# A second product of the output phase as seven inner products: A22 in blocks 2 to 6, with left sums formed a phase earlier

## The chip, the cores and the metric

The kernel runs on one core of a Trainium2 chip. The metric is the device time of one execution in microseconds. The engines are named as in the profile: PE is TensorE (matmuls; PEld its weight loads), DVE VectorE, ACT ScalarE, POOL GpSimd, SP the engine that issues most DMAs. All data are float32.

## The reference

Of the two kinds of layer that the reference knows, DEPTH = 1 leaves one: the pooling mixer, with a residual, and the final norm. x is (1, 4096, 1024).

```python
normed = rms_norm(x, norm_w)
u, gate = jnp.split(normed @ in_w, 2, axis=-1)
ug = u.reshape(b, s, 4, 256)
pooled = jnp.stack([trailing_mean(ug[:, :, g], w)
                    for g, w in enumerate((2, 4, 8, 16))], axis=2) - ug
mixed = jnp.einsum('bsgc,gcd->bsgd', pooled, group_w) + group_b
y = mixed.reshape(b, s, 1024) * scale * jax.nn.silu(gate)
h = x + y @ out_w
return rms_norm(h, final_norm_w)
```

`trailing_mean` is the mean over the last `window` tokens, fewer at the start.

## The kernel before

**Stages.** The map of each group is first multiplied into `in_w` (line L419 of the profile). Then come three phases. The first input phase ("a") takes 4 blocks of 1024 tokens and computes u and gate for channel groups 0 and 1; the second ("b") takes the same blocks for groups 2 and 3. Behind each half of a block's products `pool` forms the trailing means by a scan on VectorE, multiplies by scale, bias and gate, and stores the result y to DRAM (`yd`). The output phase ("o") takes 8 blocks of 512 tokens: y @ out_w, plus x, then the final norm and the store.

**Products.** Each matrix product of a block is cut into 2 x 2 parts and done by Winograd's form of Strassen's scheme, in seven products P1 to P7 instead of eight; the outer scheme's left sums are formed on VectorE and its right sums are formed beforehand. In the output phase they run in the order P1, P7, P6, P2, P5, P4, P3. A left factor (A11, A12, A21, A22 and sums of them) is 256 tokens by 512 channels, the right factor 512 by 512. P2 is A12 times B21; P4's left factor is A22.

**Split operands.** Every float32 factor is split into a high part, written by a ScalarE copy (L182), and a low part, the rest, by a VectorE subtract (L168). A pair of factors takes three matmuls (`mm3`, L636): high-high, high-low, low-high. One output product is 2 row halves x 4 parts of K x 3 = 24 matmuls of 128x512, the first 12 into one PSUM bank, the others into a second. The split left factors stand in a ring of four buffers, `op`.

**The inner scheme.** From block `FIRST_INNER` = 2 on, P2 is itself done as seven products of quarter size (`mm_inner`, L756): 7 x 6 = 42 matmuls of 128x256. The first, A11 x B11 of the inner scheme, stands between the two halves of P6 (`inner_first`), the other six in P2's place (`inner_rest`). The inner left sums S1 to S4 are four VectorE operations of 128x256, formed in `split_o` just before their split. The inner right sums T1 to T4 are formed by eight VectorE operations of 128x256 (`form_inner`, L168) from two raw loads, and split into slots that are retired for them (`split_inner`, tiles `inner_T`), all in block 1. `add_quarter` (L764) adds the inner products to the result on VectorE, 128x256 each.

**PSUM.** Eight banks in four sets of two: x, v, y and a free set. P1 and P2 go to x, P7 and P4 to v, P6, P5 and P3 to y; the sets change roles from block to block. `evict_o` adds a finished bank to the rows `hs` on VectorE (L1101, 128x512 an add), or, for P1, copies x into y on ScalarE. P5 writes the y banks that P6 used, with P2 between them.

**The final norm.** After P4 and after P3 `finish` squares the rows on ScalarE (L990), takes a root there, the reciprocal on VectorE (L229), and one Newton step on GpSimd (L225, L241, L242, L243, L246, all 128x2), and scales on VectorE (L994, 128x1024 each). Block 7 has a path of its own.

**What sets the order.** Each engine runs its instructions in the order in which the loop at the end of the builder issues them, held back where `tc.issue_after` says so. For step n the loop issues loads up to four products ahead (`load_reach`) on SP's queue, splits up to two ahead (`split_reach`), pooling that is due (the last two poolings fall into output block 0), then the product and its evictions. Data stand in 11 `st` and 8 `vt` slots of 128x1024 (and x2); `take` hands out the one that has been free longest.

```python
order of one step:  load -> split -> pool_due -> run (product, evict) -> load_inner, form_inner, split_inner
```

## Time and profile before

| | us |
|---|---|
| Median of 3 runs (908.23 to 908.53) | 908.41 |
| The profiled execution | 908.96 |
| Span of its trace | 907.2 |
| Output phase's first matmul of the inner scheme | 698.68 |
| End of the last matmul | 897.77 |

One more thing is worth knowing when the rows are read: DVE is VectorE, and a row such as `op<-vt,op` gives the tile written and the tiles read. The page's slices show how the load lies in time:

```profile
PE   9999999999999999999999999999999999999997
DVE  5999994894998996586696598589978888788877
POOL 0022102001100000000000000000002001001000
```

Each digit is the busy share of a fortieth of the span (22.7 us), in tenths. GpSimd has next to nothing to do from the middle of the first input phase until output block 0.

### The profile page before, as it was taken

How to read it: one execution, taken by the hardware profiler on the slowest of the kernel's cores; microseconds unless marked ns; L12 is line 12 of the kernel's file. 1: busy time of each engine (PE TensorE's matmuls, PEld its weight loads, DVE VectorE, ACT ScalarE, POOL GpSimd, SP SyncE). 2: the span in 40 equal slices, each digit the busy share in tenths (PEclk: the TensorE clock that was granted, in tenths of full speed). 3: DMA queues.
4: the chain of work that ended last, by engine and by line, in shares of the span. 5: the costliest groups of instructions: out<-in, count | busy, mean ns of one | idle time of the engine just before them, and what ended most of it. 6: DMA issues, size and time to landing. Idle time of an engine off the chain costs nothing.

```text
span 907.2 us, 11594 instructions
## 1 busy us (share of the span) xinstructions
PE 899.5 (99%) x4338; PEld 791.1 (87%) x4338; DVE 737.2 (81%) x858; ACT 471.9 (52%) x766; POOL 55.4 (6%) x129
## 2 busy tenths in 40 slices
PE   9999999999999999999999999999999999999997
PEld 7888888888888888888888888888888898898996
DVE  5999994894998996586696598589978888788877
ACT  6879547447346565256345546654435435344344
POOL 0022102001100000000000000000002001001000
PEclk9999999999999999999999999999999999999999
DMA  9984966756756535016614625745665374363332
GB/s 350 408 314 157 344 218 207 262 188 227 276 213 239 221 124 203 22 49 230 255 46 167 264 96 177 249 155 193 214 204 187 114 257 163 142 229 135 122 139 94
DMA packets 63048, 178.09 MB, mean 196 GB/s; under 512 B 6096, under 2 KB 22864, under 8 KB 62992
## 3 DMA queue, kind: packets, MB, share of 16 engines
q1 hardware_dynamic: 56496, 156.09, 47.7%
q10 hardware_dynamic: 4176, 13.65, 4.0%
q0 software_dynamic: 2320, 7.62, 2.5%
q8 instruction: 34, 0.56, 0.2%
q14 instruction: 22, 0.18, 0.1%
HBM read 116.50 MB, written 60.83 MB: 195 GB/s over the span
## 4 chain that ended last, share of the span: by engine, by line
PE 98%; DVE 1%; issue 0%; ACT 0%; DVEq 0%; ACTq 0%
PE bank L636 91%; PE bank L756 3%; PE bank L419 3%; PE bank L1208 0%; DVE w L168 0%; DVE op L168 0%; DVE st L168 0%; PE bank L485 0%; DVE vt L1073 0%; ACT vt L1021 0%; DVE vt L1101 0%; DVE st L1101 0%; ACT vt L182 0%; DVE columns L1051 0%; DVEq L1585 0%
## 5 line engine op out<-in xcount | busy, mean ns | idle before, releaser
L636 PE MATMUL bank<-op,w 128*128 128x512 f32 x2688 | 581.3, 380 | 0.1
L636 PEld LDWEIGHTS bank<-op,w 128*128 128x128 f32 x2688 | 508.6, 189 | 72.3 <-ACT early L182 0.6
L636 PE MATMUL bank<-w,op 128*128 128x512 f32 (+1 forms) x1212 | 261.2, 377 | 0.0
L636 PEld LDWEIGHTS bank<-w,op 128*128 128x128 f32 x1212 | 226.9, 189 | 30.8
L168 DVE TENSOR_TENSOR op<-st,op 128x1024 fp32r<-128x1024 f32 x124 | 150.9, 1220 | 67.8 <-ACT op L182 67.7
L182 ACT ACTIVATE op<-st 128x1024 fp32r<-128x1024 f32 x124 | 130.2, 1053 | 121.0 <-PE bank L636 83.0
L182 ACT ACTIVATE vt<-bank 128x512 f32<-128x512 f32 x98 | 55.9, 592 | 51.0 <-PE bank L636 38.7
L182 ACT ACTIVATE op<-vt 128x1024 fp32r<-128x1024 f32 x48 | 50.1, 1052 | 48.3 <-PE bank L636 22.1
L168 DVE TENSOR_TENSOR st<-st,st 128x1024 f32<-128x1024 f32 (+2 forms) x55 | 60.7, 1116 | 8.2 <-DMA st<-sd 3.3
L168 DVE TENSOR_TENSOR op<-vt,op 128x1024 fp32r<-128x1024 f32 x48 | 58.3, 1221 | 8.4 <-ACT op L182 8.3
L182 ACT ACTIVATE bank<-bank 128x512 f32<-128x512 f32 (+1 forms) x60 | 32.0, 537 | 53.0 <-PE bank L636 37.1
L1101 DVE TENSOR_TENSOR st<-bank,st 128x512 f32<-128x512 f32 x58 | 39.5, 686 | 8.0 <-PE bank L636 7.9
L225 POOL TENSOR_SCALAR oms<-oss 128x2 f32<-128x2 f32 x14 | 8.7, 620 | 591.2 <-ACT st L990 558.1
L168 DVE TENSOR_TENSOR st<-st,vt 128x1024 f32<-128x1024 f32 (+1 forms) x35 | 39.3, 1153 | 0.2
L168 DVE TENSOR_TENSOR vt<-bank,vt 128x512 f32<-128x512 f32 (+1 forms) x51 | 33.6, 681 | 6.8 <-PE bank L636 6.8
L168 DVE TENSOR_TENSOR w<-st,w 128x1024 fp32r<-128x1024 f32 x22 | 26.6, 1223 | 12.3 <-ACT w L182 12.3
L825 DVE TENSOR_TENSOR_SCAN vt<-vt,bf 128x512 f32<-128x512 f32 x28 | 34.5, 1269 | 0.2 <-ACT vt L182 0.2
L182 ACT ACTIVATE w<-st 128x1024 fp32r<-128x1024 f32 x22 | 22.9, 1052 | 17.4 <-PE bank L636 15.0
L182 ACT ACTIVATE st<-bank 128x512 f32<-128x512 f32 x32 | 18.8, 594 | 25.0 <-PE bank L636 17.8
L168 DVE TENSOR_TENSOR vt<-vt,vt 128x1024 f32<-128x1024 f32 (+1 forms) x28 | 30.7, 1102 | 1.0 <-DMA vt<-rd 0.9
L168 DVE TENSOR_TENSOR vt<-vt 128x1024 f32<-128x1024 f32 (+2 forms) x28 | 30.4, 1107 | 0.0
L182 ACT ACTIVATE st<-st 128x1024 f32<-128x1024 f32 x24 | 25.3, 1053 | 7.6 <-DVE st L168 5.4
(126 smaller groups left out, 619.9 us busy)
## 6 DMA issues: line engine op xcount, KB each, us to landing
st<-in_x SPq DMA_DIRECT2D x36, 512.0 KB, 4.5
st<-sd SPq DMA_DIRECT2D x28, 512.0 KB, 4.6
st<-in_xt SPq DMA_DIRECT2D x27, 512.0 KB, 7.6
vt<-in_x SPq DMA_DIRECT2D x21, 512.0 KB, 4.2
sd<-st ACTq DMA_DIRECT2D x21, 512.0 KB, 4.5
vt<-yd SPq DMA_DIRECT2D x18, 512.0 KB, 5.2
yd<-vt SPq DMA_DIRECT2D x17, 512.0 KB, 2.8
out<-st SPq DMA_DIRECT2D x17, 512.0 KB, 3.5
```

The lines of the kernel that those rows point to most:

```text
L168: made.append(nc.vector.tensor_tensor(out=dst, in0=a, in1=b, op=op))
L182: made.append(nc.scalar.activation(dst, src, func, **how))
L225: nc.gpsimd.tensor_scalar(out=ms, in0=ss, scalar1=1.0 / D, scalar2=EPS, op0=ALU.mult, op1=ALU.add)
L419: latest[0] = nc.tensor.matmul(ps2[kk][:, j * 256 : (j + 1) * 256], a[:, kk, 2 * j + t, :], maps if len(pairs) == 1 else woven(maps), star ...
L636: latest[0] = nc.tensor.matmul(ps, a, b, start=start and n == 0, stop=stop and n == 2, skip_group_check=True).ins
L756: latest[0] = nc.tensor.matmul(dst, a[k][x_], b[k][y_], start=start and k + n == 0, stop=k == 1 and n == 2, skip_group_check=True,).ins
L825: nc.vector.tensor_tensor_scan(s[:, j, at:end], v[:, j, at:end], v[:, j, at - win : end - win], sums_of[j] if sums_of else 0.0, ALU.add, A ...
L1101: partial["added"] = nc.vector.tensor_tensor(out=dst, in0=src, in1=dst, op=ALU.add).ins
```

## The change

The inner scheme is used for two products, by a table `INNER = {P2: (2, 7), P4: (2, 6)}` of first and last blocks: P4 (A22 times its right factor) becomes seven inner products in blocks 2 to 6. Its first inner product stands between the halves of P5 and uses the x banks, which P2 has left; its results go to the v banks.

- The inner left sums are no longer formed in `split_o`. `inner_sums`, called by `pool` in the second input phase, forms them from y for both products at once: four VectorE operations of 128x512 for each half block of tokens, for output blocks 2 to 7, and two stores to DRAM (`sumd`). The output phase loads them, one load of 512 KB per inner product, and splits them.
- `form_inner` runs on GpSimd: eight operations of 128x256 for each of the two weights, 16 in all. P4's are issued at the end of block 1, and split in block 2. T2 goes into the slot of the first raw load, T4 into columns of the weight itself (B12) that the inner scheme does not read. These columns are loaded and split again in block 7, where P4 is ordinary.
- The Newton step of the output rows: one operation is left on GpSimd, three go to VectorE (`factors`). `finish` is cut in two: `square_rows` at the eviction, and the rest one step later, behind the next operand splits.
- The loads of x come later, slots are taken by new rules, and an inner P4 is split one product ahead instead of two.

```diff
+INNER = {2: (2, 7), 4: (2, 6)}
...
-    def form_inner(m):
+    def form_inner(i, m):
...
         for k in range(2):
-            sub(dst[k], a[k], b[k])
+            nc.gpsimd.tensor_tensor(out=dst[k], in0=a[k], in1=b[k], op=ALU.subtract)
...
+    def split_inner(i, m):
+
+        src = raw_quarter(i, *{"T1": (0, 0), "T3": (0, 1), "T2": (1, 1), "T4": (1, 0)}[m])
+        if m == "T4":
+            t = b12_place(i)
+        else:
+            if m == "T2":
+                tag = st.retire_used(inner_w[i].pop(("raw", 0)))
+            else:
+                tag = st.retire()
...
+    def inner_sums(b, ys):
+
+        (a11, a21), (a12, a22) = (
+            [y.rearrange("p k (h j t) -> p h k j t", h=2, j=2)[:, :, :, j] for j in range(2)]
+            for y in ys
+        )
+        pairs_ = [take("p (q h k t) -> p q h k t", q=2, h=2, k=2) for _ in range(2)]
+        s1, s2, s3, s4 = (u[:, q] for u in pairs_ for q in range(2))
+        add(s1, a21, a22)
+        sub(s2, s1, a11)
+        sub(s3, a11, a21)
+        sub(s4, a12, s2)
+        for n, u in enumerate(pairs_):
+            nc.sync.dma_start(
+                out=sumd[b][:, n].rearrange("p q h n -> p (q h n)"),
+                in_=u.rearrange("p q h k t -> p (q h k t)"),
+            )
+            give(u)
...
         elif i == P2:
             s["12"] = load_y(b, 0, 1)
+        elif i == P5:
             load_h(b, 1)
-        elif i == P5:
+        if i == (P3 if b < NBO - 1 else P5):
             load_h(b, 0)
+        i = {P5: P2, P3: P4}.get(i)
+        if is_inner(b, i):
+            u = take("p (q k t) -> p q k t", q=4, k=2)
+            nc.sync.dma_start(
+                out=u.rearrange("p q k t -> p q (k t)"),
+                in_=sumd[b].rearrange("p n q h c -> p h (n q) c")[:, 1 if i == P2 else 0],
+            )
+            s["sums", i] = u
...
-            add(r[:, 1], a21, a22)
-            sub(r[:, 2], r[:, 1], a11)
-            sub(r[:, 3], a11, a21)
-            sub(r[:, 0], a12, r[:, 2])
...
+    def factors(b, half, ms, tmp):
+        rs = small.tile([P, ms.shape[1]], F32, tag="rs", name=f"ors{b}_{half}")
+        nc.vector.reciprocal(out=rs, in_=tmp)
+        mul(tmp, rs, ms)
+        mul(tmp, tmp, rs)
+        nc.vector.scalar_tensor_tensor(
+            out=rs, in0=tmp, scalar=1.5, in1=rs, op0=ALU.add, op1=ALU.mult
+        )
         return rs
...
+    inner_plan = {
+        (0, P3): [(load_inner, P2)],
+        (1, P1): [(form_inner, P2, m) for m in ("T1", "T3", "T2", "T4")],
+        (1, P7): [(split_inner, P2, "T1")],
+        (1, P6): [(split_inner, P2, "T3")],
+        (1, P2): [(split_inner, P2, "T2")],
+        (1, P5): [(split_inner, P2, "T4"), (end_inner, P2), (load_inner, P4)],
+        (1, P3): [(form_inner, P4, m) for m in ("T1", "T3", "T2", "T4")],
+        (2, P1): [(split_inner, P4, "T1")],
+        (2, P7): [(split_inner, P4, "T3")],
+        (2, P6): [(split_inner, P4, "T2")],
+        (2, P2): [(split_inner, P4, "T4"), (end_inner, P4)],
+        (7, P1): [(load_b12, P4)],
+        (7, P6): [(split_b12, P4)],
+    }
```

Three places show how the instructions move. First, TensorE's order in block 2 at P5 and P4 (`w_0`, `w_1` are the halves of a right factor, `op` the left one; P5's banks are 75 and 76 before, 69 and 70 after). Before:

```order
L636 MATMUL bank_75<-w_0_628,op_88 128x512 x6
L636 MATMUL bank_75<-w_1_629,op_88 128x512 x6
L636 MATMUL bank_76<-w_0_628,op_88 128x512 x6
L636 MATMUL bank_76<-w_1_629,op_88 128x512 x6
L636 MATMUL bank_73<-w_0_715,op_85 128x512 x6
L636 MATMUL bank_73<-w_1_716,op_85 128x512 x6
L636 MATMUL bank_74<-w_0_715,op_85 128x512 x6
L636 MATMUL bank_74<-w_1_716,op_85 128x512 x6
```

And now:

```order
L659 MATMUL bank_69<-w_0_634,op_88 128x512 x6
L659 MATMUL bank_69<-w_1_635,op_88 128x512 x6
L805 MATMUL bank_73<-w_0_721,op_85 128x256 x6
L659 MATMUL bank_70<-w_0_634,op_88 128x512 x6
L659 MATMUL bank_70<-w_1_635,op_88 128x512 x6
L805 MATMUL bank_75<-w_1_722,op_85 128x256 x6
L805 MATMUL bank_74<-inner_T_5112,op_86 128x256 x6
L805 MATMUL bank_75<-w_1_722,op_86 128x256 x6
L805 MATMUL bank_73<-inner_T_5034,op_86 128x256 x6
L805 MATMUL bank_76<-w_0_721,op_85 128x256 x6
L805 MATMUL bank_74<-inner_T_5069,op_86 128x256 x6
```

P4's 24 matmuls of 128x512 have become 42 of 128x256, six of them between P5's halves, and two `op` buffers feed them instead of one.

Second, VectorE's order in output block 0, where the last pooling is done and P6's and P2's banks (73 and 74, then 71) are added to the rows. Before:

```order
L168 TENSOR_TENSOR vt_106<-vt_100,vt_106 128x1024
L825 SCALAR_TENSOR_TENSOR vt_107<-vt_105,bf_0_3_1_4555 128x512
L1101 TENSOR_TENSOR st_93<-bank_73,st_93 128x512
L847 SCALAR_TENSOR_TENSOR vt_107<-vt_107,vt_105 128x2x512
L168 TENSOR_TENSOR op_88<-st_92,op_88 128x1024
L168 TENSOR_TENSOR vt_103<-vt_107,vt_103 128x1024
L1101 TENSOR_TENSOR st_95<-bank_74,st_95 128x512
L168 TENSOR_TENSOR vt_101<-st_92,vt_104 128x1024
```

And now:

```order
L188 TENSOR_TENSOR vt_100<-vt_105,vt_100 128x1024
L897 SCALAR_TENSOR_TENSOR vt_101<-vt_104,bf_0_3_1_4591 128x512
L188 TENSOR_TENSOR st_92<-vt_100 128x512
L919 SCALAR_TENSOR_TENSOR vt_101<-vt_101,vt_104 128x2x512
L1204 TENSOR_TENSOR st_99<-bank_73,st_99 128x512
L188 TENSOR_TENSOR vt_102<-vt_101,vt_102 128x1024
L1204 TENSOR_TENSOR st_96<-bank_74,st_96 128x512
L188 TENSOR_TENSOR vt_107<-vt_100,vt_102 128x512
L188 TENSOR_TENSOR op_88<-st_93,op_88 128x1024
L188 TENSOR_TENSOR vt_107<-vt_107,vt_100 128x512
L1204 TENSOR_TENSOR st_99<-bank_71,st_99 128x512
L188 TENSOR_TENSOR st_92<-vt_102,vt_107 128x512
```

The four 128x512 operations of `inner_sums` stand between the adds out of the banks.

Third, VectorE's order in block 1 around the adds that empty P7's banks (69, 70) and P6's (71, 72). Before:

```order
L1101 TENSOR_TENSOR st_90<-bank_69,st_90 128x512
L168 TENSOR_TENSOR op_88<-vt_104,op_88 128x1024
L168 TENSOR_TENSOR inner_T_4816<-vt_105,inner_T_4816 128x256 x2
L168 TENSOR_TENSOR st_91<-st_91,st_92 128x1024
L1101 TENSOR_TENSOR st_96<-bank_70,st_96 128x512
L168 TENSOR_TENSOR inner_T_4782<-vt_105,inner_T_4782 128x256 x2
L168 TENSOR_TENSOR op_85<-vt_102,op_85 128x1024
L1101 TENSOR_TENSOR st_90<-bank_71,st_90 128x512
L168 TENSOR_TENSOR inner_T_4851<-vt_107,inner_T_4851 128x256 x2
L168 TENSOR_TENSOR inner_T_4902<-vt_107,inner_T_4902 128x256 x2
L1101 TENSOR_TENSOR st_96<-bank_72,st_96 128x512
```

And now:

```order
L1204 TENSOR_TENSOR vt_106<-bank_69,vt_106 128x512
L1094 SCALAR_TENSOR_TENSOR st_91<-st_91,ors_0_4721,st_97 128x1024
L1094 SCALAR_TENSOR_TENSOR vt_103<-vt_103,ors_0_4721,st_97 128x1024
L1204 TENSOR_TENSOR vt_105<-bank_70,vt_105 128x512
L188 TENSOR_TENSOR inner_T_4792<-st_94,inner_T_4792 128x256 x2
L188 TENSOR_TENSOR inner_T_4827<-st_94,inner_T_4827 128x256 x2
L188 TENSOR_TENSOR op_85<-st_90,op_85 128x1024
L1204 TENSOR_TENSOR vt_106<-bank_71,vt_106 128x512
L188 TENSOR_TENSOR inner_T_4861<-st_92,inner_T_4861 128x256 x2
L188 TENSOR_TENSOR st_95<-vt_107,vt_100 128x1024
L1204 TENSOR_TENSOR vt_105<-bank_72,vt_105 128x512
```

Block 0's row scaling (L1094) now stands between P7's adds, and the splits of T1 and T3 (`inner_T`) ahead of the add that empties P6's first bank.

More of the change, by code (lines that the diff above doesn't have):

```diff
@@ L45, in __init__ @@
         self.used = {}
+        self.stored = set()
     def age(self):
@@ L863, in pool @@
             give(s)
-            give(sg)
+            if not q:
+                give(sg)
+        if q:
+            if 2 * b + 1 - half in sumd:
+                inner_sums(2 * b + 1 - half, sgs)
+            for sg in sgs:
+                give(sg)
     ev, evicted, copied = {}, [None], []
@@ L952, in split_o @@
         split(t, s[key])
[L953 to L962 removed]
+        if is_inner(b, i):
+            r = s.pop(("sums", i))
             t2 = next_op("p (s q k t) -> p s q k t", s=2, q=4, k=2)
@@ L976, in inverse @@
         tmp = small.tile([P, n], F32, tag="tmp", name=f"otmp{b}_{half}")
-        rs = small.tile([P, n], F32, tag="rs", name=f"ors{b}_{half}")
-        rsqrt(rs, tmp, ms, ss)
+        copy(tmp, ss, AF.Sqrt, bias=eps, scale=1.0 / D)
+        nc.gpsimd.tensor_scalar(
+            out=ms, in0=ss, scalar1=-0.5 / D, scalar2=-0.5 * EPS, op0=ALU.mult, op1=ALU.add
+        )
+        return ms, tmp
+    def factors(b, half, ms, tmp):
[5 more added lines that the diff above has]
+            out=rs, in0=tmp, scalar=1.5, in1=rs, op0=ALU.add, op1=ALU.mult
+        )
         return rs
@@ L1174, in run @@
         if kind == "o":
-            inner = b >= FIRST_INNER
-            first = (lambda: inner_first(b, split_up[n + 1], sets)) if inner and i == P6 else None
-            if inner and i == P2:
-                inner_rest(b, split_up.pop(n), sets)
+            after = step(n + 1)[2]
+            first = None
+            if n + 1 < len(steps) and is_inner(*step(n + 1)[1:]):
+                first = lambda: inner_first(after, split_up[n + 1], sets)
+            if is_inner(b, i):
+                inner_rest(b, i, split_up.pop(n), sets)
             else:
@@ L1423, in split_reach @@
             return 3
+        if kind == "o" and i == P4 and is_inner(b, i):
+            return 1
         return 2 if kind == "o" and (b, i) != (0, P1) else 1
```

184 lines of the change are left out of this document (106 added, 78 removed).

## The prediction

> **What bounds the kernel now.** I read the shares of the engines first, then the chain that ended last, then the busy time stretch by stretch. The page of the profile:
>
> ```profile
> PE 899.5 (99%) x4338; PEld 791.1 (87%) x4338; DVE 737.2 (81%) x858; ACT 471.9 (52%) x766; POOL 55.4 (6%) x129
> PE 98%; DVE 1%; issue 0%; ACT 0%; DVEq 0%; ACTq 0%
> ```
>
> The first row has TensorE busy for 899.5 of 907.2 us, the second has it holding 98% of the chain that ended last. The chain of waits, in order of time, with start, length and count:
>
> ```profile
> 59.54 639.13 PE bank L636 x2960
> 698.68 0.67 PE bank L756 x6
> 699.35 2.59 PE bank L636 x12
> 701.94 4.02 PE bank L756 x36
> 705.96 28.49 PE bank L636 x132
> ...
> 777.50 28.49 PE bank L636 x132
> ...
> 884.80 12.97 PE bank L636 x60
> 897.77 0.02 issue
> ```
>
> From 59.54 to 897.77 every piece starts where the last one ends: TensorE waits for nothing. So a matmul removed there is gained whole, but only while every other engine still arrives first; VectorE is the next bound. Its margin, stretch by stretch (columns: stretch, its length, then busy time and count of PE, PEld, DVE, ACT and POOL, granted clock, DMA share, GB/s):
>
> ```profile
> 323.15:613.20 290.05, 290.05 (x1345) 254.45 (x1345) 215.30 (x210) 148.38 (x252) 0.00 (x0) 1.00 0.43 157
> 613.20:649.50 36.30, 36.30 (x170) 31.85 (x169) 35.88 (x37) 13.03 (x29) 0.00 (x0) 1.00 0.56 190
> 649.50:670.20 20.70, 20.70 (x97) 18.16 (x96) 19.69 (x34) 12.90 (x23) 2.77 (x10) 1.00 0.79 271
> 721.50:757.30 35.80, 35.80 (x187) 31.98 (x187) 28.23 (x39) 14.72 (x23) 2.65 (x12) 1.00 0.56 195
> 757.30:793.10 35.80, 35.80 (x188) 31.97 (x187) 29.89 (x41) 14.33 (x23) 3.38 (x10) 1.00 0.50 178
> 793.10:828.80 35.70, 35.70 (x187) 31.92 (x186) 31.86 (x42) 17.21 (x26) 3.49 (x9) 1.00 0.47 169
> 828.80:864.60 35.80, 35.80 (x188) 32.00 (x187) 30.99 (x41) 14.98 (x23) 3.38 (x12) 1.00 0.45 162
> ```
>
> The second input phase (first row) leaves VectorE 74.8 us idle, and a block with the inner scheme (last four rows) about 5.5 of 35.8. In output block 0 and the first half of block 1 (second and third row) it is 99% and 95% busy: whatever lands there comes out late. The clock is 1.00 throughout.
>
> **The matmuls saved.** Block 2's pieces in the chain price both forms of a product. 132 matmuls of L636 take 28.49 us, so the 24 of an ordinary product take 24 x 28.49/132 = 5.18. The 42 of an inner product are the 6 of 0.67 and the 36 of 4.02, together 4.69. The change turns one ordinary product into an inner one in five blocks: 5 x (5.18 - 4.69) = 2.45 us less.
>
> **VectorE in blocks 2 to 6.** Rows by line and form (busy us, mean ns):
>
> ```profile
> L764 DVE TENSOR_TENSOR st<-bank,st 128x256 f32<-128x256 f32 x18 | 7.5, 417 | 3.1 <-PE bank L756 3.1
> L168 DVE TENSOR_TENSOR op<-vt,op 128x1024 fp32r<-128x1024 f32 x48 | 58.3, 1221 | 8.4 <-ACT op L182 8.3
> L168 DVE TENSOR_TENSOR vt<-vt 128x256 f32<-128x256 f32 x4 | 1.6, 419 | 0.0
> L229 DVE RECIPROCAL ors<-otmp 128x2 f32<-128x2 f32 x14 | 2.3, 162 | 1.5 <-ACT otmp L182 1.4
> ```
>
> Added per block: six quarter adds (6 x 0.417 = 2.50), one more split (1.22), six Newton instructions on two columns (nearest in size the reciprocal, 6 x 0.16 = 1.0). Removed: the four left sums (4 x 0.42 = 1.68). Net +3.0 on a mean of 30.24 in the four rows above, so 33.3 in a block that now lasts 35.78 - 0.49 = 35.29: 94%. It fits on average; what matters is the tightest hand-over. In block 4, the only one I show, VectorE empties P2's banks like this:
>
> ```profile
> 777.33 4.92 PE L636 MATMUL bank<-w,op 128*128 128x512 f32 x22
> ...
> 777.60 0.42 DVE L764 TENSOR_TENSOR vt<-bank,vt 128x256 f32<-128x256 f32 x1 [0.99 <-PE bank L756]
> 778.94 0.68 DVE L1101 TENSOR_TENSOR vt<-bank,vt 128x512 f32<-128x512 f32 x1
> ```
>
> P5 starts on TensorE at 777.50 by the chain, and its first half is 12 matmuls, 2.59 us, so P4's first inner product, which the change writes into an x bank between P5's halves, would start at 780.09. That bank's last reader is one of the adds ending at 778.94 + 0.68 = 779.62. Margin about 0.5 us, and the instructions ahead of that add in the queue are the same as now. I cost this at nothing; if the cover is gone, the price is the lateness times five.
>
> The loads of the sums, one of 512 KB for each of the eleven inner products, go out with the others on SP's queue, P2's at P1. Such a load lands so long after its issue (the page's DMA issues):
>
> ```profile
> vt<-yd SPq DMA_DIRECT2D x18, 512.0 KB, 5.2
> ```
>
> From P1's start to P2's there are three products, 15.5 us; less 5.2 for the load and at most twice the subtract's 1.22 for its split, some 8 us are left. P4's sums have a product more. Cost nothing; without that cover a late load would cost what it is late, eleven times at most.
>
> **Left sums in the second input phase.** Six calls of four 128x512 operations. No row has this shape out of SBUF with two SBUF operands in quantity; half of the 1.221 us of the 128x1024 row is 0.61, so 24 x 0.61 = 14.7 us. Four calls (blocks 2 to 5) fall into the 74.8 us of idle time, price nothing; if they met a late split each would cost at most its own 2.44. The two for blocks 6 and 7 come with the last pooling, after 613.2: 8 x 0.61 = +4.9 us into the stretch that is 99% busy.
>
> **Blocks 0 and 1, where it decides.** VectorE at the place the lateness reaches:
>
> ```profile
> 649.30 0.42 DVE L168 TENSOR_TENSOR vt<-vt 128x256 f32<-128x256 f32 x1
> ...
> 653.60 2.48 DVE L994 SCALAR_TENSOR_TENSOR st<-st,ors,st 128x1024 f32<-128x1024 f32 x2 [0.32 <-POOL ors L246]
> ...
> 658.59 2.48 DVE L994 SCALAR_TENSOR_TENSOR st<-st,ors,st 128x1024 f32<-128x1024 f32 x2 [0.64 <-POOL ors L246]
> ...
> 667.60 0.69 DVE L1101 TENSOR_TENSOR st<-bank,st 128x512 f32<-128x512 f32 x1
> 668.20 1.43 DVE L168 TENSOR_TENSOR inner_T<-vt,inner_T 128x256 fp32r<-128x256 f32 x4
> 669.53 0.69 DVE L1101 TENSOR_TENSOR st<-bank,st 128x512 f32<-128x512 f32 x1
> ```
>
> The adds at 667.60 and 669.53 empty the two banks of block 1's P6, which block 1's P5 writes next. Block 2's P2 begins its main part at 701.94; counted back through the chain, block 1 ends 60 matmuls of L636 before 698.68 (12.95 us at 0.2158), at 685.73; P5's first half then starts 72 matmuls (15.54) earlier, at 670.19, and its second half at 672.78. The adds end at 668.29 and 670.22: margins 1.9 and 2.6 us.
>
> Against that: +4.9 us (sums of blocks 6 and 7), minus the eight 128x256 forms that leave VectorE, which come before these adds. The forms start 0.34 apart where they run back to back (649.30, then an add of 0.60 between), so 8 x 0.34 = -2.7. Newton's steps add 6 x 0.16 = 1.0 in two finishes and save the 0.32 + 0.64 of waiting shown above: nought. Net +2.2, so the first add ends at 670.5 (late by 0.3). The second has T2's split ahead of it (two operations, 0.67 as 128x256 ones start) instead of four such operations, and a 128x1024 operation (1.13 between starts): 670.5 + 0.67 + 1.13 + 0.60 = 672.9 against 672.78, late by 0.1. Both are one lateness: about 0.3 us.
>
> **GpSimd's forms.** The forms are new on GpSimd: sixteen 128x256 operations with two SBUF operands, six of them (T1, T3, T2, two each) ahead of those adds through the splits that wait for them. The trace of before has no such operation. What it has is small ones, and they differ by a factor of fifteen with what VectorE does:
>
> ```profile
> 691.74 3.13 POOL L225 TENSOR_SCALAR oms<-oss 128x2 f32<-128x2 f32 x1 [6.72 <-ACT st L990]
> 695.34 0.20 POOL L242 TENSOR_TENSOR otmp<-otmp,ors 128x2 f32<-128x2 f32 x1
> ...
> 766.30 1.03 POOL L241 TENSOR_TENSOR otmp<-ors,oms 128x2 f32<-128x2 f32 x1 [1.89 <-DVE ors L229]
> ...
> 691.45 1.22 DVE L168 TENSOR_TENSOR op<-vt,op 128x1024 fp32r<-128x1024 f32 x1
> 692.59 0.76 DVE L168 TENSOR_TENSOR st<-vt 128x256 f32<-128x256 f32 x2
> 693.26 0.42 DVE L168 TENSOR_TENSOR st<-st,vt 128x256 f32<-128x256 f32 x1
> 693.59 1.22 DVE L168 TENSOR_TENSOR op<-vt,op 128x1024 fp32r<-128x1024 f32 x1
> ```
>
> An operation on two columns that takes 0.20 us took 3.13, ending at 694.87, while VectorE ran five SBUF operations back to back until 694.81. GpSimd waits for VectorE there, and a GpSimd operation under way could hold VectorE in return. Bounds for six forms: nothing, if they slip into VectorE's waits and its bank adds; and 1.03 us each, the row of a GpSimd operation that waited once, 6.2 us. By size the nearest row is VectorE's own 128x256 operation, 0.42 us, 2.5 us for six; I take half of that as falling beside bank adds and waits, 1.3 us (my choice between the bounds). Stall 0.3 + 1.3 = 1.6 us.
>
> The Trainium skill ("SBUF — State Buffer", section "Who interferes with whom") says that a VectorE operation with two SBUF inputs and a GpSimd operation that reads SBUF shut each other out; the 3.13 us row agrees for GpSimd, and no row here shows VectorE held. Its "GPSIMD Engine Reference", section "Performance versus the Vector engine", has a tensor_tensor of 2048 fp32 elements at 4497 ns; scaled to 256 my estimate is 0.56 us, 3.4 for six, and if all of it held VectorE the stall would be 3.7 and the median 909.7.
>
> **The sum.** The profiled execution took 908.96 us, 1.76 more than its span and 0.55 more than the median 908.41. 908.96 - 2.45 + 1.6 = 908.11 profiled, about **907.6** at the median. The tail after 897.77 belongs to block 7, which the new scheme leaves alone: unchanged.
>
> **Rivals.** *The full gain.* The forms slip between VectorE's operations and the 0.3 us is absorbed: stall 0 to 0.6, median 905.96 to 906.6. For it: in 649.5 to 670.2 GpSimd already did ten operations (2.77 us) with no gap on TensorE. Against it: those ten touch two columns each. Chance 0.36.
>
> *GpSimd holds VectorE, and it gets slower.* Six forms ahead of P6's adds at their upper price, 6.2 us, plus the 0.3: 6.5 us without a matmul around block 1's P5, median 908.41 - 2.45 + 6.5 = 912.5. It decides slower from a stall of 2.45 + 1.82 = 4.27 us, 0.66 per form. For it: the 3.13 us row, and the splits of T1, T3 and T2 stand in VectorE's and ScalarE's queues in order, so a form that is held keeps the operand splits behind it waiting too. Against it: VectorE's own operation of this size takes 0.42. Chance 0.19.
>
> *The hand-over of the x bank is missed in each block.* If VectorE at 94% runs over 0.5 us later at P2's end than now, TensorE waits five times; 0.36 late each is 1.8 us on top of the forecast, 909.4, at twice that 911.2. For it: 33.3 of 35.29. Against it: the queue ahead of that add starts at P2's own matmuls. Chance 0.06, half within 0.2% and half slower.
>
> **How the numbers follow.** A measurement of this kernel can tell about 0.2%, 1.8 us, from no change. Forecast 0.39, full gain 0.36, GpSimd 0.19, hand-over 0.06. Faster: 0.36, all of the full gain (its bounds lie below 908.41 - 1.82 = 906.59). Within: 0.39 + 0.03 = 0.42. Slower: 0.19 + 0.03 = 0.22. The range goes down to 905.5, the full gain less the half microsecond that the profiled run differs from the median, and up to 911.5, a stall of 5.5, which leaves the worst of the GpSimd case out. The forecast's own range is 906.6 to 910.2.
>
> **What would show it.** 210 more matmuls of the inner line and 120 fewer of the ordinary one, and steady blocks of 35.3 us, would confirm the saving; VectorE near 33 us in them its load. A gap on TensorE at the start of block 1's P5, ended by VectorE's add out of P6's bank, would confirm where it is lost, and the length of GpSimd's 128x256 operations and of the VectorE ones beside them who held whom. Gaps in every block between P5's halves would show the hand-over; none at all the full gain. The prediction is wrong altogether if TensorE waits at a place not named here: an inner operand split that comes late, or a load of sums behind stores on SP's queue.

## The result, and the profile after

The changed kernel takes **913.9 us** (median of 6 runs, 912.21 to 914.21) against 908.63 us before (6 runs, 908.23 to 909.49): ratio 1.0052, interval 1.0039 to 1.0065. It is slower by 5.3 us, 0.5%. The prediction said 907.6, in a range of 905.5 to 911.5.

The page's shares of the engines, and the shares of the chain that ended last:

```profile
PE 900.0 (99%) x4428; PEld 791.8 (87%) x4428; DVE 767.7 (84%) x937; ACT 480.2 (53%) x791; POOL 59.4 (7%) x89
PE 90%; DVE 6%; issue 2%; ACT 1%; DMA 1%; DVEq 0%; ACTq 0%
```

TensorE held 98% of that chain before; now other engines hold a tenth of it. So TensorE waits somewhere. It runs 4428 matmuls against 4338, the 90 more that 210 of the inner form and 120 fewer ordinary ones give. Its timeline from output block 0 to block 1 shows where (start, length, and in brackets the idle time ahead and what ended it):

```profile
644.68 26.14 PE L659 MATMUL bank<-w,op 128*128 128x512 f32 x120 [0.82 <-DVE st L1204]
674.31 31.75 PE L659 MATMUL bank<-w,op 128*128 128x512 f32 x132 [3.49 <-DVE vt L1204]
```

Two gaps, 0.82 us at P3 of block 0 and 3.49 us at P5 of block 1, both ended by an add that empties a bank: 4.31 us. The second row holds a further loss. Its 132 matmuls take 31.75 us. A run of 132 without a gap looks like this in the same view of the kernel before (from its start to that of the next piece it is 28.49, as the chain has it; the row counts the end of the last matmul too):

```profile
705.79 28.66 PE L636 MATMUL bank<-w,op 128*128 128x512 f32 x132
```

So 3.09 us more are lost. The windows behind the gap name the reason (stretch, its length, then PE, PEld, DVE, ACT and POOL, granted clock, DMA share, GB/s; the last row is a steady block):

```profile
665.00:670.00 5.00, 5.00 (x24) 4.37 (x24) 5.00 (x6) 1.67 (x3) 5.00 (x4) 1.00 0.43 169
670.00:675.00 5.00, 1.51 (x6) 0.98 (x5) 5.00 (x11) 2.40 (x6) 2.05 (x3) 0.86 0.73 270
675.00:680.00 5.00, 5.00 (x13) 3.93 (x12) 5.00 (x5) 0.83 (x1) 5.00 (x4) 0.50 0.60 202
680.00:685.00 5.00, 5.00 (x24) 4.34 (x23) 4.97 (x7) 1.06 (x1) 2.39 (x3) 0.96 0.27 97
764.90:800.20 35.30, 35.30 (x206) 32.08 (x205) 32.16 (x50) 16.36 (x26) 0.66 (x2) 1.00 0.60 209
```

Behind the gap the granted clock is 0.50 for five microseconds, and only 13 matmuls fit where 24 did. The steady blocks do what they should: a block lasts 35.28 us by the chain, as the starts of two like pieces show, and TensorE has no gap in it.

```profile
748.62 2.59 PE bank L659 x12
...
783.90 2.59 PE bank L659 x12
```

The account: 908.63 - 2.45 (five products) + 4.31 (gaps) + 3.09 (clock behind the second) = 913.6, against 913.9 measured. On TensorE it closes: the last 84 matmuls start at 889.58 against 884.64 before, 4.94 us later, and the three terms give 4.95. The other 0.3 us lies behind the last matmul.

What made the adds late stands on GpSimd's and VectorE's timelines. GpSimd, up to TensorE's restart:

```profile
640.69 2.17 POOL L740 TENSOR_TENSOR st<-st 128x256 f32<-128x256 f32 x2 [402.03 <-DMA st<-wod]
...
660.20 6.37 POOL L740 TENSOR_TENSOR st<-st,st 128x256 f32<-128x256 f32 x4 [1.72 <-DMA st<-wod]
666.53 5.04 POOL L740 TENSOR_TENSOR st<-st 128x256 f32<-128x256 f32 x4
```

VectorE beside them, those of its instructions that lasted longer than their kind, and the add that TensorE waited for:

```profile
641.10 1.16 DVE L188 TENSOR_TENSOR st<-vt 128x512 f32<-128x512 f32 x1
642.19 1.75 DVE L919 SCALAR_TENSOR_TENSOR vt<-vt,vt 128x1024 f32<-128x1024 f32 x1
...
660.81 1.68 DVE L188 TENSOR_TENSOR op<-st,op 128x1024 fp32r<-128x1024 f32 x1
662.41 0.68 DVE L188 TENSOR_TENSOR otmp<-ors,oms 128x2 f32<-128x2 f32 x1
...
664.15 0.69 DVE L188 TENSOR_TENSOR otmp<-otmp,ors 128x2 f32<-128x2 f32 x1
...
665.90 0.69 DVE L1068 SCALAR_TENSOR_TENSOR ors<-otmp,ors 128x2 f32<-128x2 f32 x1
...
668.30 1.75 DVE L1094 SCALAR_TENSOR_TENSOR vt<-vt,ors,st 128x1024 f32<-128x1024 f32 x1
...
670.58 1.94 DVE L188 TENSOR_TENSOR inner_T<-st,inner_T 128x256 fp32r<-128x256 f32 x4
...
673.58 0.68 DVE L1204 TENSOR_TENSOR vt<-bank,vt 128x512 f32<-128x512 f32 x1
```

An operation on two columns lasts 0.16 us elsewhere and 0.68 here; a split's subtract 1.22 and 1.68 here. The eight are longer than the same forms elsewhere (0.67, 1.21, 1.22, 0.15, 0.16, 0.16, 1.27 and 1.43 for the four) by 0.46 to 0.54 us each, 4.1 us together: nearly the two gaps. Ten forms ran in that time, and VectorE was held eight times. All eight read two operands from SBUF; the two adds out of banks beside the forms (at 666.51 and 669.98) kept their 0.68 us. GpSimd was held as well: four forms took 6.37 and 5.04 us, where a pair beside an idle VectorE takes 1.43 (a run below). And VectorE was not waiting for results: from 657.2 us to the restart it has no idle time.

### The profile page after: what moved, and what is told of

It is laid out like the page before. It is cut to its first block, busy times and chain, and to the rows that moved or that the text cites. A ratio compares the mean times of both kernels' runs of the same rounds, so it can differ in the third digit from the quotient of the medians.

```text
span 912.4 us, 11897 instructions
## 1 busy us (share of the span) xinstructions
PE 900.0 (99%) x4428; PEld 791.8 (87%) x4428; DVE 767.7 (84%) x937; ACT 480.2 (53%) x791; POOL 59.4 (7%) x89
## 4 chain that ended last, share of the span: by engine, by line
PE 90%; DVE 6%; issue 2%; ACT 1%; DMA 1%; DVEq 0%; ACTq 0%
PE bank L659 81%; PE bank L805 6%; PE bank L442 3%; DVE st L188 1%; DVE vt L897 1%; DVE op L188 1%; DVE vt L919 1%; DVE st L1204 0%; DMA early<-in_wut 0%; DVE vt L188 0%; DVE w L188 0%; ACT op L202 0%; DMA st<-in_x 0%; DVE vt L1204 0%; DVE st L1094 0%
## 5 line engine op out<-in xcount | busy, mean ns | idle before, releaser
L659 PE MATMUL bank<-w,op 128*128 128x512 f32 (+1 forms) x1092 | 240.5, 380 | 4.3 <-DVE vt L1204 3.5
L659 PEld LDWEIGHTS bank<-w,op 128*128 128x128 f32 x1092 | 205.0, 191 | 33.4 <-DVE vt L1204 3.9
L202 ACT ACTIVATE op<-vt 128x1024 fp32r<-128x1024 f32 x56 | 58.5, 1052 | 47.6 <-PE bank L659 24.9
L188 DVE TENSOR_TENSOR op<-vt,op 128x1024 fp32r<-128x1024 f32 x56 | 67.9, 1219 | 6.3 <-ACT op L202 6.3
L188 DVE TENSOR_TENSOR st<-st,st 128x1024 f32<-128x1024 f32 (+1 forms) x52 | 60.5, 1178 | 8.5 <-DMA st<-sd 2.9
L1204 DVE TENSOR_TENSOR vt<-bank,vt 128x512 f32<-128x512 f32 x58 | 39.3, 683 | 3.2 <-PE bank L659 3.2
L188 DVE TENSOR_TENSOR vt<-bank,vt 128x512 f32<-128x512 f32 x50 | 33.0, 686 | 6.7 <-PE bank L659 6.7
L188 DVE TENSOR_TENSOR w<-st,w 128x1024 fp32r<-128x1024 f32 (+1 forms) x28 | 31.2, 1125 | 7.2 <-ACT w L202 7.1
L805 PE MATMUL bank<-w,op 128*128 128x256 f32 x264 | 36.6, 275 | 0.0
L805 PEld LDWEIGHTS bank<-w,op 128*128 128x128 f32 x264 | 34.6, 192 | 1.2
L202 ACT ACTIVATE w<-st 128x1024 fp32r<-128x1024 f32 (+1 forms) x28 | 26.6, 961 | 16.6 <-PE bank L659 12.5
L740 POOL TENSOR_TENSOR st<-st 128x256 f32<-128x256 f32 x8 | 9.1, 1154 | 402.0 <-DMA st<-wod 402.0
```

Source lines behind the costliest of these rows:

```text
L188: made.append(nc.vector.tensor_tensor(out=dst, in0=a, in1=b, op=op))
L202: made.append(nc.scalar.activation(dst, src, func, **how))
L659: latest[0] = nc.tensor.matmul(ps, a, b, start=start and n == 0, stop=stop and n == 2, skip_group_check=True).ins
L740: nc.gpsimd.tensor_tensor(out=dst[k], in0=a[k], in1=b[k], op=ALU.subtract)
L805: latest[0] = nc.tensor.matmul(dst, a[k][x_], b[k][y_], start=start and k + n == 0, stop=k == 1 and n == 2, skip_group_check=True,).ins
L1204: partial["added"] = nc.vector.tensor_tensor(out=dst, in0=src, in1=dst, op=ALU.add).ins
```

## The experiments

The theory, A: a form on GpSimd holds VectorE for half a microsecond, VectorE has no room in blocks 0 and 1, and a long gap drops TensorE's clock on top. Its main rival, B: VectorE is late by itself, through the sums of blocks 6 and 7. All times of rows are those of one profiled execution, the others are medians. Each run is compared with runs of the kernel before on the same chip (their medians 908.55 to 908.87 us).

**Forms left out.** The GpSimd operations go; loads and splits stay.

```diff
-        for k in range(2):
-            nc.gpsimd.tensor_tensor(out=dst[k], in0=a[k], in1=b[k], op=ALU.subtract)
```

> The changed kernel with the forming of the inner right sums T1 to T4 left out (16 GpSimd operations; the raw parts are split in their place, so the output is not the reference's). Theory A, GpSimd's forms hold VectorE: in the changed kernel eight VectorE operations before TensorE's restart at 674.3 us are longer by 0.46 to 0.54 us each beside a form, 4.1 us in all, of 4.3 us of gaps. Without forms the gaps shrink to 0.3 us or less, TensorE's granted clock does not drop, and the time is 908.6 - 2.45 + 0.25 = about 906.4 us. Theory B, VectorE is late by itself through the sums of blocks 6 and 7 (eight operations, 4.8 us) and the forms only fall into that wait: a gap of 3 us or more stays, 911 us or more.

Measured 907.01 us (906.77 to 907.40), ratio 0.9982 (0.9973 to 0.9991), 6.9 us below the changed kernel. One gap is left:

```profile
670.39 28.76 PE L659 MATMUL bank<-w,op 128*128 128x512 f32 x132 [0.53 <-DVE vt L1202]
```

0.53 us, and the 132 matmuls behind it at full clock. VectorE runs the same operations in the same order here, and those that were long have their usual length (the last row is the add that ends the gap):

```profile
659.93 1.21 DVE L188 TENSOR_TENSOR op<-st,op 128x1024 fp32r<-128x1024 f32 x1
661.05 0.16 DVE L188 TENSOR_TENSOR otmp<-ors,oms 128x2 f32<-128x2 f32 x1
...
665.38 1.28 DVE L1092 SCALAR_TENSOR_TENSOR vt<-vt,ors,st 128x1024 f32<-128x1024 f32 x1
...
667.18 1.42 DVE L188 TENSOR_TENSOR inner_T<-st,inner_T 128x256 fp32r<-128x256 f32 x4
...
669.65 0.68 DVE L1202 TENSOR_TENSOR vt<-bank,vt 128x512 f32<-128x512 f32 x1
```

All eight together are 4.1 us shorter than in the changed kernel, and the gaps are 3.8 us shorter. B falls: the sums alone cost half a microsecond. 908.55 - 2.45 + 0.53 + 0.10 (the row's 28.76 against 28.66) = 906.7.

**Forms back on VectorE, at their place.**

```diff
-            nc.gpsimd.tensor_tensor(out=dst[k], in0=a[k], in1=b[k], op=ALU.subtract)
+            sub(dst[k], a[k], b[k])
```

> The changed kernel with the forms back on VectorE, at the same place. Theory A: 4.1 us of holding go, 8 x 0.34 = 2.7 us of VectorE work come ahead of the add that empties P6's first bank, and the order that results puts the splits of T1 and T3 (1.4 us) behind it, so one gap of about 1.6 us is left at block 1's P5 and none in block 0; if a gap of that length leaves the clock alone, about 907.8 us. Theory B, VectorE's own load decides: 2.7 us more on it make it later than in the changed kernel, 914 us or more.

Measured 909.90 us (908.07 to 910.89), ratio 1.0013 (1.0004 to 1.0022): 4 us better than the changed kernel with 2.7 us more on VectorE in block 1, so B falls again. TensorE's rows:

```profile
666.88 33.51 PE L659 MATMUL bank<-w,op 128*128 128x512 f32 x154 [0.89 <-DVE op L188]
715.70 0.94 PE L805 MATMUL bank<-inner_T,op 128*128 128x256 f32 x6 [1.38 <-ACT bank L202]
```

The gap in block 1 is 0.89 us (1.6 expected), and it stands elsewhere: at the start of P2, where TensorE waits for an operand split; P5 has none. One of 1.38 us is new in block 2, which I had not foreseen. It goes back to a load of inner left sums that came late: ScalarE copies from it at 712.25, VectorE's split and an add follow, then the copy that TensorE waits for.

```profile
712.25 2.02 ACT L202 ACTIVATE op<-vt 128x1024 fp32r<-128x1024 f32 x2 [6.86 <-DMA vt<-sumd]
```

What held that load up is not shown. The time is 2 us over the expected one, and the gaps account for 0.7 of it.

**Sums of blocks 6 and 7 in the output phase.** They are formed in `split_o` from the loaded y, as before, and no sums are stored for these blocks.

```diff
-    b: dram.tile([P, 2, 2, 2, 2 * P], F32, name=f"sumd{b}") for b in range(FIRST_INNER, NBO)
+    b: dram.tile([P, 2, 2, 2, 2 * P], F32, name=f"sumd{b}") for b in range(FIRST_INNER, 6)
...
+                add(r[:, 0], a21, a22)
+                sub(r[:, 1], r[:, 0], a11)
+                sub(r[:, 2], a11, a21)
+                sub(r[:, 3], a12, r[:, 1])
```

> The changed kernel with the inner left sums of blocks 6 and 7 formed in the output phase again, as before, in place of the last two poolings; forms stay on GpSimd. Theory A: VectorE in blocks 0 and 1 has 4.8 us less, the forms still hold it for some 4 us, lateness 0.25 + 4.1 - 4.8 = below nothing, no gap there; block 6's VectorE has 2.7 us more on 32.2 of 35.3 us and just fits: 906.2 to 907.2 us. Rival C, the splits of T1 and T3 wait for GpSimd's results and block the queue whatever VectorE's load is: a gap of 3 us or more stays, 911 us or more.

Measured 910.01 us (908.94 to 911.96), ratio 1.0014 (1.0005 to 1.0022). Neither answer: gaps of 1.44, 0.56, 1.41 and 0.18 us, two of them here:

```profile
647.96 13.22 PE L659 MATMUL bank<-w,op 128*128 128x512 f32 x60 [1.44 <-DVE st L1215]
...
673.77 2.86 PE L659 MATMUL bank<-w,op 128*128 128x512 f32 x12 [1.41 <-DVE vt L1215]
```

The profiled execution is the slowest of the eleven, 911.96 us. With 4.8 us less to do VectorE is no longer full: it is busy for 2.35 of the 5 us from 670 to 675. So the second gap is not its load; its timeline there shows it idle for 1.77 us without a cause that the profile names, and for 0.88 until a load of y lands. Eight forms ran on GpSimd by 645.1, ahead of the first gap. There rival C's mechanism does show: the split of T1 stands in ScalarE's queue and waits for GpSimd's result, and VectorE's next scan waits 1.36 us for ScalarE.

```profile
636.97 0.42 ACT L202 ACTIVATE inner_T<-st 128x256 fp32r<-128x256 f32 x1 [1.36 <-POOL st L740]
```

In the changed kernel no row of ScalarE names a form as what it waited for up to the restart. The expectation of no gap was wrong, and the run does not tell the theories apart.

**Forms on VectorE, held behind P6's adds of block 1**, and the splits of T1 to T4 behind them.

```diff
+            with tc.issue_after(partial["added"]):
+                sub(dst[k], a[k], b[k])
...
+        (1, P6): [(form_inner, P2, m) for m in ("T1", "T3", "T2", "T4")],
+        (1, P2): [(split_inner, P2, "T1"), (split_inner, P2, "T3")],
```

> The changed kernel with the forms on VectorE and held behind P6's adds of block 1, where VectorE had 6.8 us idle before (8.70 busy of 15.50), the splits of T1 to T4 behind them. Theory A: VectorE loses the 4.1 us of holding and 2.0 us of splits ahead of the adds, no gap at block 1's P5, 908.6 - 2.45 = 906.2 us, up to 906.8. Theory B: the sums of blocks 6 and 7 alone make the adds late, 909 us or more. Rival D: the work behind the adds makes the next adds or T1's use late, a new gap after 674 us, 907 us or more.

Measured 909.55 us (909.26 to 910.34), ratio 1.0011 (1.0002 to 1.0020).

```profile
670.04 28.82 PE L659 MATMUL bank<-w,op 128*128 128x512 f32 x132 [0.18 <-DVE vt L1205]
703.51 0.94 PE L806 MATMUL bank<-inner_T,op 128*128 128x256 f32 x6 [0.72 <-ACT bank L202]
711.22 0.94 PE L806 MATMUL bank<-w,op 128*128 128x256 f32 x6 [1.50 <-DVE vt L1205]
```

The gap in block 1 is down to 0.18 us, as A has it; but rival D came true as well: P4's forms now make VectorE late at block 2's P2, 2.2 us.

**Forms in the second input phase.** T1 to T4 are formed on VectorE in its last block, stored, and only loaded later.

```diff
+        ("b", 3, P1): [(load_inner, P2, wod)] + [(form_inner, P2, m) for m in all_t],
+        ("b", 3, P2): [(store_inner, P2)],
+        ("b", 3, P6): [(load_inner, P4, wod)] + [(form_inner, P4, m) for m in all_t],
+        ("b", 3, P7): [(store_inner, P4)],
```

> The changed kernel with T1 to T4 of both products formed on VectorE in the last block of the second input phase (16 operations of 128x256, two loads and two stores of 512 KB per product) and only loaded in the output phase; nothing is left out. Theory A: VectorE has idle time there, and without forms in blocks 0 and 1 one gap of 0.53 us is left, as in the run with the forms left out: 907.0 us, 906.5 to 907.5. Rival E: the run without forms was fast because the waits for the forms were gone too, and loads, stores and slots held longer in the second input phase make splits late there: a gap before 613 us, 908 us or more.

Measured 912.51 us (910.03 to 913.42), ratio 1.0037 (1.0026 to 1.0048). Rival E's gap before 613 us is there, and a longer one comes in block 0, where the last poolings start later: the first scan at 614.86, 3.7 us later than in the run with the forms left out (611.18), with TensorE only 1.1 us later there:

```profile
572.45 41.49 PE L662 MATMUL bank<-op,w 128*128 128x512 f32 x191 [0.58 <-DVE op L188]
647.40 56.31 PE L662 MATMUL bank<-w,op 128*128 128x512 f32 x252 [2.38 <-DVE st L1214]
```

At 28.49/132 us a matmul, and 0.17 for the end of the last, 252 matmuls take 54.56 us, so 1.75 us are lost to the clock behind a gap of 2.38. At block 1's P5 there is no gap. Whether the late loads or the forms themselves hold things up is not separated: ScalarE waits 4.84 us for a weight at 576.42, and VectorE has no idle time from 555 to 585 us, with the sixteen forms in between.

**The same, with the unread half of block 7's sums left out.**

```diff
+        h = slice(1, 2) if b == NBO - 1 else slice(0, 2)
```

> As the run with the forms in the second input phase, and the left sums of block 7 formed for P2 alone (its P4 is ordinary and never reads the other half): four operations of 128x256 in place of 128x512 ahead of block 1, 4 x (0.60 - 0.34) = 1.0 us less on VectorE. Theory A, VectorE's load ahead of P6's adds decides to the tenth of a microsecond: the gap of 0.53 goes, 0.5 us faster than that run, 906.5 us. If the gap stays, it is not VectorE's load that sets it.

Measured 911.85 us (909.82 to 914.66), ratio 1.0037 (1.0022 to 1.0051). The gaps are 0.45 and 2.85 us at the two places of the run before; at block 1's P5 neither run has one, so the question could not be answered here.

**The kernel before, delayed**, by three and by five needless VectorE operations.

```diff
+        if b == 1 and i == P6:
+            u = take("p (a b) -> p a b", a=2)
+            with tc.issue_after(partial["added"]):
+                for _ in range(3):
+                    sub(u, hs[b][1, 0], hs[b][1, 1])
+            give(u)
```

> The kernel before with three needless VectorE operations of 128x1024 ahead of the adds that empty P6's banks in block 1 (reading rows that are there, into a spare slot). Their margin of 1.9 us is used up: 3 x 1.13 = 3.4, and an add of another bank that the order puts ahead, 0.6: gap about 2.1 us. If only the gap counts, 908.6 + 2.1 = 910.7 us. If a gap makes TensorE's granted clock drop afterwards, as behind the gap of 3.49 us of the changed kernel (0.50 for 5 us), and not as behind its gap of 0.82 us (1.00), the time tells on which side 2.1 us lies: some 3 us more, 914 us.

> As with three operations, with five: gap about 4.3 us. If only the gap counts, 908.6 + 4.3 = 912.9 us; if the clock drops behind a gap of this length as in the changed kernel (the 132 matmuls after it took 31.75 us in place of 28.49), 916 us, and the windows behind the gap show the granted clock at about 0.5.

Measured 909.95 us (909.60 to 910.49), ratio 1.0014 (1.0006 to 1.0023), with three; 914.68 us (914.42 to 914.82), ratio 1.0066 (1.0052 to 1.0081), with five. TensorE with three:

```profile
671.02 28.76 PE L636 MATMUL bank<-w,op 128*128 128x512 f32 x132 [1.22 <-DVE st L1107]
```

And with five, and the window behind the gap:

```profile
674.12 30.17 PE L636 MATMUL bank<-w,op 128*128 128x512 f32 x132 [4.43 <-DVE st L1107]
```
```profile
675.00:680.00 5.00, 5.00 (x20) 4.17 (x20) 4.56 (x8) 0.00 (x0) 0.00 (x0) 0.80 0.40 137
```

The short gap (1.22 us, 2.1 expected) costs itself and 0.10 us: 908.62 + 1.22 + 0.10 = 909.94. The long one costs itself and 1.51 us of clock: 908.62 + 4.43 + 1.51 = 914.6. So a late VectorE is enough, with no form on GpSimd and no inner P4, to bring a gap, the dropped clock behind it and a loss of this size.

**The kernel before with its forms on GpSimd**, nothing else.

```diff
-            sub(dst[k], a[k], b[k])
+            nc.gpsimd.tensor_tensor(out=dst[k], in0=a[k], in1=b[k], op=ALU.subtract)
```

> The kernel before with nothing changed but that the eight forms of P2's right sums run on GpSimd. Theory A: each form holds VectorE for about 0.5 us where it has two operands in SBUF, 4 us for eight, against 2.7 us of work that leaves VectorE: P6's adds in block 1 come about 1.4 us later against a margin of 1.9, so the time hardly moves, 908.6 to 909.2 us, and some eight VectorE operations beside the forms last 0.45 to 0.55 us longer than their kind. If VectorE's operations keep their usual length, GpSimd does not hold it and the theory falls.

Measured 910.13 us (909.70 to 910.69), ratio 1.0013 (1.0004 to 1.0023), a gap of 1.11 us at block 1's P5. GpSimd's rows, then VectorE's:

```profile
645.86 4.29 POOL L714 TENSOR_TENSOR vt<-vt 128x256 f32<-128x256 f32 x2 [406.42 <-DMA yd<-vt]
...
653.90 1.43 POOL L714 TENSOR_TENSOR vt<-vt 128x256 f32<-128x256 f32 x2
```
```profile
646.59 1.22 DVE L168 TENSOR_TENSOR op<-vt,op 128x1024 fp32r<-128x1024 f32 x1
...
656.76 2.48 DVE L994 SCALAR_TENSOR_TENSOR st<-st,ors,st 128x1024 f32<-128x1024 f32 x2 [3.66 <-POOL ors L246]
...
662.83 2.48 DVE L994 SCALAR_TENSOR_TENSOR st<-st,ors,st 128x1024 f32<-128x1024 f32 x2 [0.93 <-POOL ors L246]
```

My expectation failed in its mechanism. VectorE's operations keep their length; it is GpSimd that is held, two forms for 4.29 us, where two run in 1.43 with VectorE idle. The price comes by another road: Newton's steps of the row norm stand behind the forms in GpSimd's queue, and VectorE waits 3.66 us for the first of them, where it waited 0.32 before. (A second wait, 0.93 us against 0.64 before, comes when the forms are long done.) This is also what the changed kernel avoids by moving those steps to VectorE.

**P4 ordinary, all else as changed.**

```diff
-INNER = {2: (2, 7), 4: (2, 6)}
+INNER = {2: (2, 7)}
```

> The changed kernel with P4 ordinary again (no forms, splits or inner products for it), all else as changed. The steady blocks give back 2.45 us. P2's eight forms run on GpSimd at the same place as before P6's adds. Theory A: the lateness is nearly that of the changed kernel, less the two forms of P4 that fell ahead of the restart: gaps of 3 to 4 us and the clock behind them, 908.6 + 3 to 4 + 2 to 3 = 914 to 916 us. Rival F, the second product's own work (its raw loads and slots in block 1) made the adds late: gaps under 1 us, 909.5 us or less.

Measured 915.17 us (913.05 to 915.99), ratio 1.0064 (1.0050 to 1.0077): A, and rival F falls. TensorE's rows of the profiled run:

```profile
644.73 26.14 PE L659 MATMUL bank<-w,op 128*128 128x512 f32 x120 [0.82 <-DVE st L1204]
673.80 28.76 PE L659 MATMUL bank<-w,op 128*128 128x512 f32 x132 [2.93 <-DVE vt L1204]
```

The second gap is 0.56 us shorter than the changed kernel's. Here seven VectorE operations are long and not eight: the four splits at 670.59 take 1.42 us, and the two forms of P4 that ran beside them are gone. The gap follows the count of the holds. In this execution, 913.05 us, the clock did not drop (28.76); the three others, 914.85 to 915.99 us, have a lower mean clock (0.995 to 0.997 against 0.998); they were not profiled, so the drop in them is likely but not shown.

**Two versions meant to be faster.** Forms on VectorE behind P6's adds (P2) and behind block 2's P2 (P4); P4 inner from block 3; the unread halves of the sums left out. Then the same with the forms spread, two or four operations a step:

```diff
-INNER = {2: (2, 7), 4: (2, 6)}
+INNER = {2: (2, 7), 4: (3, 6)}
...
+        (1, P6): [(form_inner, P2, "T1"), (form_inner, P2, "T3")],
+        (1, P2): [(form_inner, P2, "T2"), (form_inner, P2, "T4"), (split_inner, P2, "T1")],
...
+        (2, P5): [(form_inner, P4, "T1")],
+        (2, P4): [(form_inner, P4, "T3"), (split_inner, P4, "T1")],
+        (2, P3): [(form_inner, P4, "T2"), (split_inner, P4, "T3")],
+        (3, P1): [(form_inner, P4, "T4"), (split_inner, P4, "T2")],
```

> Forms on VectorE behind P6's adds of block 1 (P2) and behind P2's adds of block 2 (P4), where VectorE has room; P4 inner in blocks 3 to 6 only, so that P4's forms no longer fall ahead of block 2's P2, where the run with the forms behind P6 had gaps of 0.72 and 1.50 us; the unread half of the left sums of blocks 2 and 7 not formed. Saved 4 x 0.49 = 1.96 us; gap at block 1's P5 0.18 less 1.0, nothing. Theory A: 908.6 - 1.96 = 906.7 us, up to 907.2. Rival D, that work only pushes the lateness to the next place: a gap of 1 us or more in blocks 1 to 3 and 908 us or more.

> As the run with the forms late and P4 inner from block 3, with the forms spread: P2's four operations a step behind P6's and P2's adds of block 1, P4's two a step from block 2's P5 to block 3's P1, so that no eight of them stand ahead of one bank add. Theory A, each gap is VectorE's queue ahead of that bank's add: the 0.63 us at block 2's P5 goes, the 0.30 us at block 2's P6 shrinks, 908.7 - 1.96 + 0.3 = 907.0 us. Rival D: the same work makes another add late, gaps of 0.9 us in all and 908.4 us or more.

The first: 908.84 us (907.63 to 910.23), ratio 0.9999 (0.9991 to 1.0008), 1.6 us over A's upper end, and neither answer fits. The gaps are 0.30 and 0.63 us, the first behind 2.95 us in which VectorE was idle without a cause that the profile names, the second behind eight forms in a row:

```profile
705.83 10.63 PE L659 MATMUL bank<-w,op 128*128 128x512 f32 x48 [0.30 <-DVE st L1209]
717.08 18.37 PE L659 MATMUL bank<-w,op 128*128 128x512 f32 x84 [0.63 <-DVE st L1209]
```

Spread, it takes **907.51 us** (907.08 to 908.72), ratio 0.9988 (0.9979 to 0.9997): 1.2 us faster than the kernel before, just clear of the noise, and TensorE's waits in the trace hold no add any more. Rival D falls. In the profiled execution TensorE has the whole 1.96 us that four inner products save (its last 84 matmuls start at 882.63 against 884.64); at the median 1.2 are left, and what takes the rest is not shown.

## Why the prediction was wrong

**The bound and the saving: right.** TensorE sets the time, and five inner products save 5 x (35.77 - 35.28) = 2.45 us.

**VectorE in blocks 2 to 6: right.** 33.3 us a block was predicted, 32.16 measured, and the bank of P4's first inner product was free in time in every block: there is no gap behind the one at 674.31.

**Left sums in the second input phase: right.** No gap there; the 128x512 operations take 0.68 us and start 0.60 apart (0.61 predicted).

**VectorE's lateness without GpSimd: right in kind, 0.2 us off.** 0.3 us was worked out, and the run with the forms left out has a gap of 0.53.

**GpSimd's forms: the step that failed.** The forecast put the stall at 1.6 us, 1.3 of it for the forms; the gaps were 4.31 us, and with the clock 7.4. "By size the nearest row is VectorE's own 128x256 operation, 0.42 us, 2.5 us for six; I take half of that as falling beside bank adds and waits, 1.3 us." Little fell beside other work: of ten forms eight held VectorE for 0.51 us on average, 4.1 us. Three things were off. The discount of a half had no row behind it: VectorE was 95% busy there before, and that speaks against free places. Ten forms ran ahead of the restart, not six, since T4 and P4's first came early. And the count began too late: two ran in block 0, where P3's bank had a margin that the working never looked at, and made the gap of 0.82 us. The upper bound, 6.2 us, would have held the 4.1.

**The clock: no term at all.** The sum took a gap to cost its own length. The 3.49 us gap cost 3.09 us more. Without this the time would have been about 910.5 us (908.63 - 2.45 + 4.31), inside the range, but still slower where 0.8 us faster was forecast: the forms are the first error, the clock the second.

**The rivals.** The GpSimd rival, chance 0.19, named the mechanism, the place and the direction; its threshold (a stall of 4.27 us, 0.66 a form) was just reached by the gaps (4.31), with more forms at a lower price each. The chance was too low: what spoke for it, the row of 3.13 us, showed GpSimd waiting for VectorE and left the reverse open, and what spoke against it was only the size of VectorE's own operation. The Trainium skill ("SBUF — State Buffer", section "Who interferes with whom") says that issue order and not the shape of the operation decides which of the two is blocked. The runs agree as to the shape: the same forms held VectorE eight times in the changed kernel and not once in the kernel before with its forms moved, and GpSimd was held in both. What makes the order come out one way or the other was not settled. The estimate from the Trainium skill's "GPSIMD Engine Reference", section "Performance versus the Vector engine", 0.56 us for a form, was nearer to the measured 0.51 us of holding than my choice, 0.22 us a form; a form alone takes 0.7.

The full gain and the missed hand-over did not come.

## What to carry to other kernels

Moving work to an idle engine costs the busy engine whatever the two share: price it at full, for every operation that can run before the deadline, unless a stretch of the profile shows room, and look at what stands behind it in the idle engine's queue. A tuned kernel's margins are for each bank and each deadline: list all deadlines in the crowded stretch, not the one that looks nearest, and place bursts of work behind them in small pieces (the spread forms made the 0.63 us gap vanish). And of the gaps on TensorE measured here, those up to 1.5 us cost 0.1 us or so beyond their length, while those from 2.4 us on cost up to 3.1 us more.

## What the runs showed of the hardware

**The price of a gap.** The granted clock after a gap, by the time of the 132 matmuls that follow it (28.66 us without one, in the same view):

| run | gap, us | 132 matmuls, us |
|---|---|---|
| before, three operations more | 1.22 | 28.76 |
| changed, P4 ordinary (profiled execution) | 2.93 | 28.76 |
| changed | 3.49 | 31.75 |
| before, five operations more | 4.43 | 30.17 |

The loss does not grow with the gap: 2.93 us was all but free in one execution while 2.38 us cost 1.75 in another kernel. It goes with the time at half clock. In windows of 1 us the changed kernel's clock is below 1.00 from here to here:

```profile
673.00:674.00 1.00, 0.00 (x0) 0.00 (x0) 1.00 (x2) 1.00 (x3) 0.00 (x0) 0.79 0.71 266
...
680.00:681.00 1.00, 1.00 (x5) 0.85 (x4) 1.00 (x3) 0.00 (x0) 1.00 (x2) 0.80 1.06 375
```

If it steps between 1.00 and 0.50, it stood at 0.50 from 673.58 to 680.40, 6.8 us. The same working gives 3.4 us for the kernel before with five operations more and 3.4 us for each of the two runs with the forms in the second input phase. So the half rate came in one stretch of 3.4 us or in two, and cost some 1.5 to 1.8 or 3.1 us. The Trainium skill ("TensorE: Matmul & The Clock Gate", section "Part 1: The HAM clock gate (the "warmup" mystery)") has a clock at half rate after an idle window of about 3.4 us, full again after a busy one, with windows that run freely, so that it depends on where a gap falls in them. The half rate (0.50 in the window of the changed kernel), the length of 3.4 us and the recovery agree, and the free gap of 2.93 us fits the chance in it; the drop behind gaps of 2.38 and 2.85 us came sooner than a full window of idleness. The two groups among the changed kernel's runs (912.21 and 912.61; 913.88 to 914.21) are as such a chance would have it, but only one run, of the slower group, was profiled.

**GpSimd and VectorE.** A GpSimd subtract of 128x256 with two operands in SBUF runs in about 0.7 us alone (1.43 for two) and held eight VectorE operations of the changed kernel for 0.46 to 0.54 us each, even those that work on two columns and take 0.16 by themselves. In the kernel before with its forms moved it held none.
